# A dilated attention merge whose weights travel through DRAM instead of through TensorE

## The chip, the cores and the metric

The kernel runs on one core of a Trainium2 chip. The metric is the device time of one execution in microseconds. The core has a matrix engine (TensorE, PE in the profile), three engines for elementwise work (VectorE is DVE, ScalarE is ACT, GpSimd is POOL), a sync engine (SP) that issues the transfers, and 16 DMA engines that carry them out.

## The reference

The program is one layer of an encoder on 1024 positions of width 1024, in float32. What matters here is branch A, a dilated sliding-window attention with 8 heads of 64. It runs three window patterns, and merges them per position and head by their softmax denominators:

```python
def mixture_of_dilations(q, k, v, rel_bias):
    outs, lses = [], []
    for window, dilation in DIL_PATTERNS:          # (128,1), (512,4), (2048,16)
        o, lse = dilated_window_attention(q, k, v, rel_bias, window, dilation)
        outs.append(o)
        lses.append(lse)
    w = jax.nn.softmax(jnp.stack(lses, axis=0), axis=0)
    return jnp.einsum('gbsh,gbshd->bshd', w.astype(q.dtype), jnp.stack(outs, axis=0))
```

Branch B is a 2-D neighbourhood attention with 8 heads. Both branches are gated, projected and added to the residual; a feed-forward part with a depthwise convolution follows.

## The kernel before

Matrix products are made exact enough by splitting each float32 operand into a high and a low part, so one product step is three matmuls of 128x512 (lines L84 to L86, `product`). The program has these stages: a start with norms and the first projections, an attention loop, a gate stage, and the feed-forward part. The change lies in the attention loop.

**The slot loop.** The loop has 101 slots. Its order for TensorE, VectorE and ScalarE is written out by hand: `at(slot, phase, job)` puts a job into a slot, and each slot runs its phases in the order `first`, `O`, (fill), `T`, (fill), `late O`, `S`, `last`, (fill), `W`. Fill steps are product steps of the input projection, four in each of the slots 0 to 63, eight in 64 to 71, six in 72 to 87 and four after that; while they run, queued side work (evictions of results, splits of weights) is emitted as well. SP and GpSimd are not in that written order: a planner orders their instructions by its own simulation.

**The heads.** Dilated heads run in four pairs. Pair `pr` begins in slot 16·pr with its first head; the second head starts eight slots later. A pair's rows of the outputs `u` hold head 0 on partitions 0 to 63 and head 1 on 64 to 127. The pattern (128,1) is called near (group `g` = 0, tile `u1`), and the two dilated patterns are computed together and called far (`g` = 1, tile `u23`). Scores are made in `S`, the softmax (`softmax`, L580 and L581) runs on VectorE and ScalarE, the probabilities are transposed on TensorE in `T` into one of two PSUM buffers named T, and `split_t` (L588, L589) takes them out as high and low parts; a slot later they are multiplied with the values into a buffer O, which `finish` moves to `u`. Neighbourhood heads (`NaHead`) follow from slot 64 on, one each four slots, beside the end of pair 3.

**The merge.** The softmax leaves in `st` a negated maximum and a sum for each query row, for near (indices 0 and 1) and far (2 and 3). Near and far hold the queries in different orders on the partitions. Before the change this is how the weights come about:

- `exchange` (L799, slots 13 to 16 of the pair): 16 VectorE copies of 32x8 bring far's statistics into near's order, in `xs`.
- `factors` (L807 to L810, slot 16) and `shares` (L815 to L820, slot 17): the two weights per query, in `fa`.
- `give` (L825, slots 18 to 21): 16 VectorE copies bring far's weights back into far's order, in `fx`.
- `spread` (L830): GpSimd writes a quarter's weights 64 times, as `fw`, 128x512.
- `weigh` (L838, L840; slots 20, 21, 23, 24, phase `W`): TensorE transposes `fw` in four 128x128 blocks into a T buffer, and VectorE multiplies a quarter of `u` by it.
- `merge` (L847, L848, slot 25): GpSimd adds near to far, SP stores the pair to DRAM.

Of the kernel before, what the change touches and what calls it, by code (L numbers as in the profile page):

```python
# [10 lines left out]
FT = mybir.dt.float32  # L11
FR = mybir.dt.float32r
AF = mybir.ActivationFunctionType
OP = mybir.AluOpType
# [3 lines left out]
S = 1024  # L18
# [11 lines left out]
def hybrid_encoder(tc, xT, c, w_ada, small, w_in, p1_bias, p23_bias, na_bias, ln2_mult, ident, w_br, w_out,  # L30
                   w_up, w_down, out):
    nc = tc.nc
    act, dve, pool, pe, sp = nc.scalar, nc.vector, nc.gpsimd, nc.tensor, nc.sync
# [3 lines left out]
    dram = tc.alloc_tile_pool(name="scr", bufs=1, space=DRAM)  # L37
# [4 lines left out]
    idt = const.tile([128, 128], FT, name="idt")  # L42
# [186 lines left out]

    vb_c = dram.tile([S, 512], FT, name="vbc")  # L230
    g_scr = dram.tile([16, 128, S], FT, name="gs")
    o_scr = [dram.tile([4, 128, S], FT, name=n) for n in ("oa", "ob")]
    v_scr = dram.tile([S + 9 * 128, 512], FT, name="v")
    va_s, va_b = v_scr[:S], v_scr[S:].rearrange("(j p) n -> j p n", j=9)
# [147 lines left out]
    with tc.manual_schedule(engines={e.engine for e in (sp, act, dve, pool, pe)}):  # L382
        x = [x_load(0)]
# [16 lines left out]
        first = ps_s.tile([128, 512], FT, name="pv", bufs=3)  # L400
# [99 lines left out]
        for n, step in enumerate(v_steps[:9]):  # L500
# [14 lines left out]
            else:  # L515
                p = v_wide(*step[1:])
# [62 lines left out]
    def softmax(d, bias, pp, mi, li):  # L579
        dve.tensor_tensor_reduce(pp, d, bias, -1.0, BIG, OP.add, OP.min, mi)  # L580
        act.activation(pp, pp, AF.Exp, bias=mi, scale=-1.0, accum_out=li)  # L581
# [63 lines left out]
    def at(slot, phase, job, *args):  # L645
        slots[slot][phase].append((job, args))

    class DilHead:
# [22 lines left out]
        def load(self):  # L671
            loads[self.head] = dil_loads(self.head)
# [8 lines left out]
        def far_scores(self, r):  # L681
            qs, ks, kl, qb = qks[self.pr]
            ensure(qk_marks[self.pr])
            i, st = self.i, self.st()
            s = ps_l.tile([128, 512], FT, name="S")
            P = self.P[r] = sm_pool.tile([128, 2, 256], FT, name="P", bufs=5)
            for g in range(2):
                d = s[:, 256 * g:256 * g + 256]
                qc = slice(256 * r + 128 * g, 256 * r + 128 * g + 128)
                kc = slice(256 * r, 256 * r + 256)  # L690
                pe.matmul(d, qs[i][:, qc], ks[i][:, kc], start=True, stop=False)
                pe.matmul(d, qs[i][:, qc], kl[i][:, kc], start=False, stop=True)  # L692
            for g in range(2):
                d = s[:, 256 * g:256 * g + 256]
                e = 2 * r + g
                softmax(d, self.bt[:, 640 - 128 * g:896 - 128 * g], P[:, g], st[:, i, 2, e:e + 1], st[:, i, 3, e:e + 1])

        def far_turn(self, r):
            P = self.P.pop(r)
# [20 lines left out]
        def near_scores(self, n):  # L720
            qs, ks, kl, qb = qks[self.pr]
            ensure(qk_marks[self.pr])
            i, st = self.i, self.st()
            s = ps_l.tile([128, 512], FT, name="S")
            P = sm_pool.tile([128, 2, 256], FT, name="P", bufs=5)
            for x_ in range(2):
                b = 2 * n + x_
                t0, t1 = block_chunks(b)[0]
                d = s[:, 256 * x_:256 * x_ + 256]
                mid = t0 is not None and t1 is not None  # L730
                for dd, *keys in [(d, t0, 2)] if mid else [(d[:, 0:128], t0), (d[:, 128:256], t1)]:
                    pe.matmul(dd, qb[i][:, 128 * b:128 * b + 128], window(ks[i], *keys), start=True, stop=False)
                    pe.matmul(dd, qb[i][:, 128 * b:128 * b + 128], window(kl[i], *keys), start=False, stop=True)
            for x_ in range(2):
                b = 2 * n + x_
                off = block_chunks(b)[1]
                softmax(s[:, 256 * x_:256 * x_ + 256], self.bt[:, off:off + 256], P[:, x_], st[:, i, 0, b:b + 1],
                        st[:, i, 1, b:b + 1])
                self.P["near", b] = P[:, x_]

        def near_turn(self, js):
# [31 lines left out]
    class DilPair:  # L773
        def __init__(self, pr):
            self.pr, s0 = pr, 16 * pr
            at(s0, "first", self.begin) if pr else self.begin()
            for i in range(2):
                DilHead(self, pr, i, s0 + 8 * i, lambda: self.u, lambda: self.st)
            for r in range(4):
                at(s0 + 13 + r, "first", self.exchange, r)  # L780
                at(s0 + 18 + r, "first", self.give, r)
            at(s0 + 16, "last", self.factors)
            at(s0 + 17, "last", self.shares)
            for n, (g, z) in enumerate(((0, 0), (0, 1), (1, 0), (1, 1))):
                s = s0 + 18 + n + g
                at(s, "last", self.spread, g, z)
                at(s + 2, "W", self.weigh, g, z)
            at(s0 + 25, "first", self.merge)

        def begin(self):  # L790
            self.u = [at_pool.tile([128, S], FT, name=n) for n in ("u1", "u23")]
            self.st = sm_pool.tile([128, 2, 4, 8], FT, name="st")
            self.fw = {}

        def exchange(self, r):
            if r == 0:
                self.xs = at_pool.tile([128, 2, 2, 8], FT, name="xs")
            for q in range(4):
                dve.tensor_copy(self.xs[32 * r:32 * r + 32, :, :, q:8:4],  # L799
                                self.st[32 * q:32 * q + 32, :, 2:4, 2 * r:2 * r + 2])  # L800

        def factors(self):
            st, xs = self.st, self.xs
            fa = at_pool.tile([128, 2, 2, 8], FT, name="fa")
            fb = at_pool.tile([128, 2, 2, 8], FT, name="fb", bufs=1)
            fl = at_pool.tile([128, 2, 8], FT, name="fl", bufs=1)
            dve.tensor_tensor(fl, st[:, :, 0], xs[:, :, 0], OP.min)  # L807
            dve.tensor_tensor(fa[:, 0], fl, st[:, :, 0], OP.subtract)
            dve.tensor_tensor(fa[:, 1], fl, xs[:, :, 0], OP.subtract)
            act.activation(fa, fa, AF.Exp)  # L810
            self.fa, self.fb, self.fl = fa, fb, fl

        def shares(self):
            st, xs, fa, fb, fl = self.st, self.xs, self.fa, self.fb, self.fl
            dve.tensor_tensor(fb[:, 0], fa[:, 0], st[:, :, 1], OP.mult)  # L815
            dve.tensor_tensor(fb[:, 1], fa[:, 1], xs[:, :, 1], OP.mult)
            dve.tensor_tensor(fl, fb[:, 0], fb[:, 1], OP.add)
# [3 lines left out]
            self.fac = [fa[:, 0], at_pool.tile([128, 2, 8], FT, name="fx")]  # L821

        def give(self, r):
            for q in range(4):
                dve.tensor_copy(self.fac[1][32 * q:32 * q + 32, :, 2 * r:2 * r + 2],  # L825
                                self.fa[32 * r:32 * r + 32, 1, :, q:8:4])

        def spread(self, g, z):
            fw = self.fw[g, z] = at_pool.tile([128, 4, 2, 64], FT, name="fw")
            pool.tensor_scalar(fw, self.fac[g][:, :, 4 * z:4 * z + 4].rearrange("p i b -> p b i")  # L830
                               .rearrange("p b (i o) -> p b i o", o=1).to_broadcast([128, 4, 2, 64]), 1.0, None, OP.mult)

        def weigh(self, g, z):
            fw = self.fw.pop((g, z))
            ensure(self.done)
            pt = ps_a.tile([128, 512], FT, name="T")
            for b in range(4):
                pe.transpose(pt[:, 128 * b:128 * b + 128], fw[:, b], idt)  # L838
            dst = self.u[g][:, 512 * z:512 * z + 512]
            return lambda: dve.tensor_tensor(dst, dst, pt, OP.mult)  # L840

        def merge(self):
            u = self.u
# [8 lines left out]
    class NaHead:  # L852
# [15 lines left out]

        def load(self):
            if self.i == 0:  # L870
                oTs[self.head // 2] = at_pool.tile([128, S], FT, name="u1")
            self.st = at_pool.tile([128, 2, 8], FT, name="stb")
            self.vv = v_raw(vb_load, self.head)

# [896 lines left out]
```

## Time and profile before

| What | Value |
|---|---|
| Time, three runs | 1532.61, 1534.29, 1536.65 us; median 1534.29 |
| Profiled execution | 1535.67 us, of which its span is 1533.8 us |
| Busy, TensorE | 1494.4 us (97%) |
| Busy, VectorE | 994.6 us (65%) |
| Busy, ScalarE | 771.6 us (50%) |
| Busy, GpSimd | 774.2 us (50%) |
| DMA, mean over the span | 134 GB/s |

The profile is one execution. Its span runs from the first to the last instruction; the rest of the time lies around it. A row of a view names the line of the kernel, the engine, the operation, and the tiles written and read; in brackets may stand how long the engine was idle before it and who released it. PEld is the loading of weights into TensorE, which overlaps its matmuls. SPq is SP's queue; its rows give the time that an issue takes, not the transfer.

### The profile page before, as it was taken

The numbers are of one execution on the slowest core, as the hardware profiler recorded it, in microseconds if no ns is written. First come the engines' busy times: TensorE is split into PE (matmuls) and PEld (weight loads), VectorE is DVE, ScalarE is ACT, GpSimd is POOL, SyncE is SP. The second block draws the span as 40 slices with busy tenths as digits, with TensorE's granted clock in tenths as the row PEclk, the third lists the DMA queues.
The fourth block names the chain that finished last, engine by engine and source line by source line (L and its number), as shares of the span: only waits on it lengthen the run. The fifth ranks groups of instructions, "written<-read, shape, count | busy, mean of one in ns | idle before, by whom it ended". The sixth has DMA issues, their size and how long they took to land.

```text
span 1533.8 us, 21797 instructions
## 1 busy us (share of the span) xinstructions
PE 1494.4 (97%) x7740; PEld 1267.5 (83%) x7740; DVE 994.6 (65%) x1892; ACT 771.6 (50%) x1439; POOL 774.2 (50%) x640
## 2 busy tenths in 40 slices
PE   8999999999999999999999989999999998999998
PEld 7888888889798998878888867888888887778787
DVE  5775357575656655646525798766666668787765
ACT  4331566666656566643335463444444447475542
POOL 1021344443335444512268578676666666779721
PEclk9999999999999999999999999999999999999999
DMA  9567333333625456477644222222222224513313
GB/s 349 191 242 258 93 107 82 108 90 102 185 83 150 128 143 173 149 246 234 213 137 147 88 69 96 82 98 88 85 84 86 86 78 154 191 62 124 117 55 111
DMA packets 112725, 205.77 MB, mean 134 GB/s; under 512 B 40516, under 2 KB 53188, under 8 KB 112580
## 3 DMA queue, kind: packets, MB, share of 16 engines
q1 hardware_dynamic: 112344, 204.12, 41.2%
q8 instruction: 61, 1.00, 0.3%
q14 instruction: 48, 0.39, 0.1%
q10 hardware_dynamic: 272, 0.26, 0.1%
HBM read 159.25 MB, written 42.47 MB: 132 GB/s over the span
## 4 chain that ended last, share of the span: by engine, by line
PE 50%; POOL 8%; DVE 7%; ACT 3%; issue 3%; DMA 3%; DVEq 0%; POOLq 0%; ACTq 0%
PE pj L1204 8%; PE pj L1205 8%; PE pj L1206 8%; PE pj L84 6%; PE pj L86 6%; PE pj L85 6%; POOL wsl L61 2%; DMA wraw<-w_down 2%; PE pj L365 2%; PE O L932 2%; POOL wlo L61 2%; DVE big L1426 1%; PE T L919 1%; PE S L897 1%; DVE kl L340 1%
## 5 line engine op out<-in xcount | busy, mean ns | idle before, releaser
L61 POOL TENSOR_TENSOR wlo<-wraw,whi 128x512 fp32r<-128x512 f32 (+1 forms) x94 | 116.1, 1256 | 173.6 <-ACT whi L57 155.4
L84 PE MATMUL pj<-h,whi 128*128 128x512 f32 x448 | 186.7, 417 | 2.6 <-ACT h L207 2.2
L85 PE MATMUL pj<-h,whi 128*128 128x512 f32 x448 | 176.5, 394 | 2.1 <-DVE h L209 2.1
L86 PE MATMUL pj<-h,wlo 128*128 128x512 f32 x448 | 176.3, 393 | 0.0
L61 POOL TENSOR_TENSOR wsl<-big,wsh 128x512 fp32r<-128x512 f32 (+1 forms) x86 | 116.6, 1376 | 43.4 <-ACT wsh L57 43.4
L639 POOL TENSOR_TENSOR wlo<-wraw,whi 128x512 fp32r<-128x512 f32 x58 | 74.7, 1298 | 118.4 <-ACT whi L638 118.4
L589 DVE TENSOR_TENSOR tl<-T,th 128x512 fp32r<-128x512 f32 (+3 forms) x120 | 77.1, 653 | 72.9 <-ACT th L588 71.4
L581 ACT ACTIVATE P<-P,st 128x256 f32<-128x256 f32 x128 | 64.2, 502 | 95.9 <-DVE st L580 95.9
L1426 DVE SCALAR_TENSOR_TENSOR big<-wc,sm,big 128x256 f32<-128x256 f32 (+1 forms) x129 | 101.0, 827 | 15.1 <-ACT big L1420 15.1
L86 PEld LDWEIGHTS pj<-h,wlo 128*128 128x128 f32 x448 | 84.3, 188 | 18.7
L84 PEld LDWEIGHTS pj<-h,whi 128*128 128x128 f32 x448 | 85.0, 190 | 14.3 <-ACT h L207 2.8
L85 PEld LDWEIGHTS pj<-h,whi 128*128 128x128 f32 x448 | 85.0, 190 | 13.4 <-DVE h L209 3.4
L57 ACT ACTIVATE whi<-wraw 128x1024 fp32r<-128x1024 f32 (+2 forms) x51 | 49.5, 972 | 69.8 <-PE pj L85 26.7
L61 POOL TENSOR_TENSOR wsl<-wraw,wsh 128x384 fp32r<-128x384 f32 (+1 forms) x46 | 53.6, 1184 | 58.4 <-ACT wsh L57 58.3
L910 POOL TENSOR_SCALAR P<-P,stb 128x288 f32<-128x288 f32 (+1 forms) x32 | 40.2, 1255 | 72.2 <-DVE stb L907 64.7
L1426 DVE SCALAR_TENSOR_TENSOR big<-pj,sm,big 128x512 f32<-128x512 f32 (+1 forms) x129 | 66.4, 563 | 15.7 <-ACT big L1420 15.7
L588 ACT ACTIVATE th<-T 128x512 fp32r<-128x512 f32 (+3 forms) x120 | 65.6, 566 | 20.4 <-PE T L919 14.0
L57 ACT ACTIVATE wsh<-big 128x1024 fp32r<-128x1024 f32 (+1 forms) x43 | 42.9, 997 | 57.3 <-POOL big L1155 43.0
L547 POOL TENSOR_TENSOR vv<-vv 128x512 fp32r<-128x512 f32 (+1 forms) x40 | 41.9, 1065 | 47.2 <-ACT vv L546 47.2
L580 DVE CUSTOM_DVE_ANT_0 P<-S,bias 128x256 f32<-128x256 f32 x128 | 48.9, 419 | 21.4 <-PE S L692 17.0
L903 ACT ACTIVATE P<-P,stb 128x288 f32<-128x288 f32 (+1 forms) x64 | 36.4, 569 | 50.3 <-DVE stb L901 50.2
L1225 DVE TENSOR_TENSOR pj<-pj,wc 128x512 f32<-128x512 f32 x33 | 22.9, 695 | 53.1 <-PE pj L1206 53.1
(431 smaller groups left out, 4814.3 us busy)
## 6 DMA issues: line engine op xcount, KB each, us to landing
wraw<-w_in SPq DMA_DIRECT2D x34, 512.0 KB, 4.3
wada<-w_ada SPq DMA_DIRECT2D x31, 512.0 KB, 8.0
big<-w_up SPq DMA_DIRECT2D x22, 512.0 KB, 5.4
wraw<-w_up SPq DMA_DIRECT2D x22, 512.0 KB, 3.7
as<-big SPq DMA_DIRECT2D x22, 512.0 KB, 2.8
big<-as SPq DMA_DIRECT2D x22, 512.0 KB, 6.7
wraw<-w_down SPq DMA_DIRECT2D x24, 384.0 KB, 3.6
gs<-gs SPq DMA_DIRECT2D x32, 256.0 KB, 2.9
```

The source lines that it names most:

```text
L57: act.activation(hi, raw, AF.Copy)
L61: lo_eng.tensor_tensor(lo[:, i:i + step], raw[:, i:i + step], f(hi)[:, i:i + step], OP.subtract)
L84: pe.matmul(psum, whi[:, k0 + k], mhi, start=k == 0, stop=False)
L85: pe.matmul(psum, whi[:, k0 + k], mlo, start=False, stop=False)
L86: pe.matmul(psum, wlo[:, k0 + k], mhi, start=False, stop=k == n - 1)
L588: act.activation(th[:m, :n], pt[:m, :n], AF.Copy)
L589: dve.tensor_tensor(tl[:m, :n], pt[:m, :n], f(th)[:m, :n], OP.subtract)
L639: pool.tensor_tensor(lo[:, i:i + n], raw[:, i:i + n], f(hi)[:, i:i + n], OP.subtract)
L1204: pe.matmul(psum, whi[:, k], bhi, start=j < 4 and k == 0, stop=False, skip_group_check=True)
L1205: pe.matmul(psum, whi[:, k], blo, start=False, stop=False, skip_group_check=True)
L1206: pe.matmul(psum, wlo[:, k], bhi, start=False, stop=k == n - 1, skip_group_check=True)
L1426: dve.scalar_tensor_tensor(y[:, dst], src, wt, y[:, dst], OP.mult, OP.add)
```

## The change

The merge's weights no longer pass through VectorE copies, GpSimd and TensorE. Instead:

- `st` is laid out with the statistic first, and in slot 17 one TensorE transpose (`turn`) turns it to 64 rows of 128. `rows` copies them out of PSUM; SP stores them to a DRAM scratch (`st_scr`) and loads them back as `fs`, 64 partitions of 32 positions each, with nine loads that bring near and far into one order.
- `factors` and `shares` compute on 64x32 and move to slots 20 and 21. Afterwards `fa` goes to a second DRAM scratch (`f_scr`) with nine stores.
- A quarter's weights come back as `fb`, 128x512, by a transfer that reads each of the two heads' rows 64 times. Two buffers exist: far's quarters are loaded after `shares`, and near's as the far quarters free the buffers.
- `weigh` is one VectorE multiply of `u` by `fb`, in the phase `last` of slots 24, 26, 28 and 30, far first; `merge` moves from slot 25 to slot 31.
- `exchange`, `give` and `spread` are gone. The neighbourhood outputs, which took `u1` buffers, now take `u1` and `u23` in turn.

```diff
-                softmax(d, ..., st[:, i, 2, e:e + 1], st[:, i, 3, e:e + 1])
+                softmax(d, ..., st[:, 2, i, e:e + 1], st[:, 3, i, e:e + 1])
...
-            for r in range(4):
-                at(s0 + 13 + r, "first", self.exchange, r)
-                at(s0 + 18 + r, "first", self.give, r)
-            at(s0 + 16, "last", self.factors)
-            at(s0 + 17, "last", self.shares)
-            for n, (g, z) in enumerate(((0, 0), (0, 1), (1, 0), (1, 1))):
-                s = s0 + 18 + n + g
-                at(s, "last", self.spread, g, z)
-                at(s + 2, "W", self.weigh, g, z)
-            at(s0 + 25, "first", self.merge)
+            at(s0 + 17, "T", self.turn)
+            at(s0 + 20, "last", self.factors)
+            at(s0 + 21, "last", self.shares)
+            for n, (g, z) in enumerate(((1, 0), (1, 1), (0, 0), (0, 1))):
+                at(s0 + 24 + 2 * n, "last", self.weigh, g, z)
+            at(s0 + 31, "first", self.merge)
...
+        def turn(self):
+            pt = ps_a.tile([128, 512], FT, name="T")
+            pe.transpose(pt[:64, :128], self.st.rearrange("p s i b -> p (s i b)"), idt)
+            return lambda: self.rows(pt)
+
+        def rows(self, pt):
+            rows = at_pool.tile([64, 128], FT, name="fs", bufs=1)
+            dve.tensor_copy(rows, pt[:64, :128])
+            sp.dma_start(st_scr[self.pr], rows)
+            self.fs = at_pool.tile([64, 4, 32], FT, name="fs", bufs=1)
+            sp.dma_start(self.fs[:, 2:4], st_scr[self.pr][32:64].rearrange("(s x) (q j) -> (x q) s j", s=2, j=32))
+            near = st_scr[self.pr][0:32].rearrange("(s i b) (r j) -> i r b s j", s=2, i=2, r=4)
+            for i in range(2):
+                for r in range(4):
+                    sp.dma_start(self.fs[32 * i + 8 * r:32 * i + 8 * r + 8, 0:2], near[i, r])
...
+            to = f_scr[self.pr]
+            sp.dma_start(to[1].rearrange("i (x j) -> (i x) j", j=32), fa[:, 1])
+            near = to[0].rearrange("i (b r j) -> i r b j", b=8, r=4)
+            for i in range(2):
+                for r in range(4):
+                    sp.dma_start(near[i, r], fa[32 * i + 8 * r:32 * i + 8 * r + 8, 0])
+            self.fb = {}
+            for z in range(2):
+                self.load(1, z)
+
+        def load(self, g, z):
+            fb = self.fb[g, z] = at_pool.tile([128, 512], FT, name="fb")
+            sp.dma_start(fb, f_scr[self.pr, g][:, 512 * z:512 * z + 512].rearrange("i (o n) -> i o n", o=1)
+                         .to_broadcast([2, 64, 512]))
 
         def weigh(self, g, z):
-            fw = self.fw.pop((g, z))
             ensure(self.done)
-            pt = ps_a.tile([128, 512], FT, name="T")
-            for b in range(4):
-                pe.transpose(pt[:, 128 * b:128 * b + 128], fw[:, b], idt)
             dst = self.u[g][:, 512 * z:512 * z + 512]
-            return lambda: dve.tensor_tensor(dst, dst, pt, OP.mult)
+            dve.tensor_tensor(dst, dst, self.fb.pop((g, z)), OP.mult)
+            if g:
+                self.load(0, z)
```

More of the change, by code (lines that the diff above doesn't have):

```diff
@@ L231, in hybrid_encoder @@
     g_scr = dram.tile([16, 128, S], FT, name="gs")
+    st_scr = dram.tile([4, 64, 128], FT, name="sts")
+    f_scr = dram.tile([4, 2, 2, S], FT, name="fcs")
     o_scr = [dram.tile([4, 128, S], FT, name=n) for n in ("oa", "ob")]
@@ L695, in far_scores @@
                 e = 2 * r + g
[L696 removed]
+                softmax(d, self.bt[:, 640 - 128 * g:896 - 128 * g], P[:, g], st[:, 2, i, e:e + 1], st[:, 3, i, e:e + 1])
         def far_turn(self, r):
@@ L793, in begin @@
[L793 to L800, printed above, removed]
-        def factors(self):
[L803 to L809, printed above, removed]
+            self.st = sm_pool.tile([128, 4, 2, 8], FT, name="st")
@@ L810, in factors @@
+        def factors(self):
+            fs = self.fs
+            self.fa = fa = at_pool.tile([64, 2, 32], FT, name="fa", bufs=1)
+            self.fl = fl = at_pool.tile([64, 32], FT, name="fl", bufs=1)
+            dve.tensor_tensor(fl, fs[:, 0], fs[:, 2], OP.min)
+            for g in range(2):
+                dve.tensor_tensor(fa[:, g], fl, fs[:, 2 * g], OP.subtract)
             act.activation(fa, fa, AF.Exp)
-            self.fa, self.fb, self.fl = fa, fb, fl
         def shares(self):
-            st, xs, fa, fb, fl = self.st, self.xs, self.fa, self.fb, self.fl
@@ L815, in shares @@
-            dve.tensor_tensor(fb[:, 0], fa[:, 0], st[:, :, 1], OP.mult)
-            dve.tensor_tensor(fb[:, 1], fa[:, 1], xs[:, :, 1], OP.mult)
-            dve.tensor_tensor(fl, fb[:, 0], fb[:, 1], OP.add)
+            fs, fa, fl = self.fs, self.fa, self.fl
+            for g in range(2):
+                dve.tensor_tensor(fs[:, 2 * g], fa[:, g], fs[:, 2 * g + 1], OP.mult)
+            dve.tensor_tensor(fl, fs[:, 0], fs[:, 2], OP.add)
             dve.reciprocal(fl, fl)
@@ L870, in load @@
             if self.i == 0:
-                oTs[self.head // 2] = at_pool.tile([128, S], FT, name="u1")
+                oTs[self.head // 2] = at_pool.tile([128, S], FT, name=("u1", "u23")[self.head // 2 % 2])
             self.st = at_pool.tile([128, 2, 8], FT, name="stb")
```

14 lines of the change are left out of this document (2 added, 12 removed).

## The prediction

> **What bounds the kernel now.** I read the page first, for the engine that sets the end, then slices of the trace stage by stage, because the share of an engine over the whole span says nothing about the one stage that is edited.
>
> ```profile
> span 1533.8 us, 21797 instructions
> ...
> PE 1494.4 (97%) x7740; PEld 1267.5 (83%) x7740; DVE 994.6 (65%) x1892; ACT 771.6 (50%) x1439; POOL 774.2 (50%) x640
> ...
> PE 50%; POOL 8%; DVE 7%; ACT 3%; issue 3%; DMA 3%; DVEq 0%; POOLq 0%; ACTq 0%
> ```
>
> TensorE is 97% busy and carries half of the chain that ended last. Nothing else can shorten this kernel except through what TensorE is given to do or what it waits for. So each step below is priced by what it does to TensorE.
>
> The edited work lies in slots 12 to 24 of each head pair. In slots 0 to 63 a slot holds four fill steps of 12 wide matmuls in all, so the first wide matmul of every twelfth marks a slot's start. I counted them and asked for the same six slots at the same phase of the 16-slot period: slots 4 to 9, where no merge runs yet, and the six that hold a merge's weighing in pair 0 (20 to 25), pair 1 (36 to 41) and pair 2 (52 to 57). Columns: window, its length, busy time and count of TensorE, its weight loads, VectorE, ScalarE and GpSimd, granted clock, DMA share, GB/s.
>
> ```profile
> 173.50:198.90 25.40, 25.40 (x151) 22.00 (x150) 13.59 (x38) 17.47 (x45) 12.01 (x11) 1.00 0.32 84
> 242.10:269.90 27.80, 27.66 (x168) 23.51 (x166) 20.21 (x57) 17.98 (x46) 15.56 (x14) 1.00 0.29 75
> 313.10:340.90 27.80, 27.65 (x168) 23.50 (x166) 20.22 (x57) 17.98 (x46) 16.05 (x15) 1.00 0.28 74
> 384.20:415.30 31.10, 28.26 (x168) 23.29 (x167) 21.73 (x57) 19.74 (x45) 11.88 (x9) 1.00 0.62 169
> 469.80:510.20 40.40, 39.80 (x244) 35.12 (x245) 23.28 (x63) 21.34 (x50) 20.40 (x17) 1.00 0.52 149
> 528.60:561.30 32.70, 32.53 (x206) 29.07 (x205) 18.96 (x49) 20.60 (x46) 16.52 (x14) 1.00 0.64 184
> ```
>
> The first row is the price without the merge: 25.4 us. With it: 27.8, 27.8 and 31.1. Pair 3 is weighed in slots 68 to 72, beside neighbourhood heads (40.4 us); slots 76 to 80 are the same heads without it (32.7 us), with two fill steps fewer in each of four slots. The clock is 1.00 throughout, so these are waits and instructions, not throttling.
>
> **What the merge costs on TensorE, and so what leaves.** A close look at one group of four transposes, at a lone transpose, and at a wait:
>
> ```profile
> 246.00 0.39 PE L85 MATMUL pj<-h,whi 128*128 128x512 f32 x1
> ...
> 246.23 0.39 PE L86 MATMUL pj<-h,wlo 128*128 128x512 f32 x1
> ...
> 246.46 0.60 PE L838 MATMUL T<-idt,fw 128*128 128x128 f32 x4
> ...
> 247.13 0.40 PE L85 MATMUL pj<-h,whi 128*128 128x512 f32 x1
> ...
> 247.90 0.42 PEld L703 LDWEIGHTS T<-idt,P 128*128 128x128 f32 x4 [0.57 <-DVE tl L589]
> ```
>
> ```profile
> 232.77 0.39 PE L86 MATMUL pj<-h,wlo 128*128 128x512 f32 x1
> ...
> 233.00 0.27 PE L749 MATMUL T<-idt,P 128*128 128x128 f32 x1
> ...
> 233.35 0.40 PE L85 MATMUL pj<-h,whi 128*128 128x512 f32 x1
> ```
>
> ```profile
> PEld T L749 <- DVE tl L589: 3.0, 3, 2.1
> ```
>
> Wide matmuls start 0.23 us apart when nothing is between them (246.00, 246.23). From 246.23 to 247.13 lie two such steps and the group: 0.90 - 0.46 = 0.44 us for four transposes. The lone one: 0.58 - 0.46 = 0.12 us. The wait of 0.57 us at 247.90 is the second cost: a weighing takes one of the two T buffers, so the next slot's transposes must wait until VectorE has split the previous slot's. Without the weighing they need the buffer of two slots back. The last row (who waited for whom, 384 to 416 us) is the same wait in pair 2, longest 2.1 us.
>
> - Pairs 0 and 1: 27.8 - 25.4 = 2.4 us by the windows, 2.3 by the unrounded starts. 4 x 0.44 = 1.8 of it are transposes, the rest T waits. All of it goes: 2 x 2.3 = 4.6 us.
> - Pair 2: 31.1 - 25.4 = 5.7 us. 1.8 are transposes and about 3 T waits; the remainder follows slow strided evictions that stay. I take 4.2; ends 1.8 and 5.7.
> - Pair 3: the eight extra fill steps cost 8 x 3 x 0.23 = 5.5 us, so 40.4 - 32.7 - 5.5 = 2.2 us. I take 2.2; ends 1.8 and 2.6.
> - Added: one transpose per pair (`turn`), 0.12 us by the lone row, at most a group's 0.44: 4 x 0.12 = 0.5 us. It stands in slot 17 with two other T users, but those buffers were split a slot earlier.
>
> On TensorE: 4.6 + 4.2 + 2.2 - 0.5 = 10.5 us less.
>
> **What leaves and comes on VectorE and GpSimd.**
>
> ```profile
> L799 DVE COPY xs<-st x64: 162/167/306, 213.6 to 441.2; 32x8 f32<-32x8 f32 x64
> L825 DVE COPY fx<-fa x64: 146/161/1797, 235.8 to 479.9; 32x4 f32<-32x4 f32 x64
> L830 POOL TENSOR_SCALAR fw<-fx x8: 1485/1491/1505, 248.2 to 487.2; 128x512 f32<-128x512 f32 x8
> L840 DVE TENSOR_TENSOR u<-u,T x16: 673/684/687, 248.4 to 508.7; 128x512 f32<-128x512 f32 x16
> L1171 DVE TENSOR_TENSOR big<-big 128x512 f32<-128x512 f32 x10 | 15.9, 1589 | 1.2 <-POOL big L1155 1.2
> 268.33 0.69 DVE L589 TENSOR_TENSOR tl<-T,th 128x512 fp32r<-128x512 f32 x1 [1.22 <-ACT th L588]
> 271.14 0.68 DVE L624 TENSOR_TENSOR u<-O,u 64x512 f32<-64x512 f32 x1 [1.44 <-ACT u L623]
> ```
>
> 32 copies a pair leave VectorE (at least 32 x 0.16 = 5 us), and four spreads of 1.49 us leave GpSimd. Neither is on the path, as the 25.4 us row shows with VectorE only 13.6 us busy, so I book nothing for them; their room covers what comes. The factor arithmetic keeps its kind and shrinks to 64x32, about 0.17 us each. `rows` adds one small copy, hidden in VectorE's idle stretches of 1.2 to 1.4 us a slot (last two rows).
>
> The four weighings a pair stay on VectorE, but their second operand now comes from SBUF instead of PSUM. L840 has 0.68 us with T; L1171, with both operands in SBUF while GpSimd works, 1.59. I take 0.9 us, since GpSimd is busy 14 of 28 us here. The 0.2 us more per quarter fits in the idle stretches: nothing on TensorE; at worst 16 x 0.9 = 14.5 us of VectorE time, a quarter of which might show.
>
> The Trainium skill, "SBUF — State Buffer", section "SBUF: two separate sides", says that a VectorE operation with two SBUF inputs and a GpSimd operation that reads SBUF lock each other out for a whole instruction. By that rule, which speaks against this edit, a weighing could wait a whole GpSimd instruction; the L1171 row agrees.
>
> **The two round trips through DRAM.** They matter only if VectorE stands waiting, since all that is queued behind it (softmax, the split of T, evictions) feeds TensorE a slot later.
>
> ```profile
> 118.00:120.50 2.50, 2.50 (x12) 2.05 (x12) 2.40 (x5) 0.00 (x0) 0.00 (x0) 1.00 0.43 184
> ```
>
> ```profile
> out<-x SPq DMA_DIRECT2D x8, 128.0 KB, 1.9
> bias<-p_bias SPq DMA_DIRECT2D x8, 256.0 KB, 2.7
> ```
>
> ```profile
> 230.99 0.69 DVE L589 TENSOR_TENSOR tl<-T,th 128x512 fp32r<-128x512 f32 x1 [0.78 <-ACT th L588]
> ...
> 237.31 1.20 SPq L484 DMA_DIRECT2D vv<-v  x2
> ...
> 248.10 0.42 DVE L580 CUSTOM_DVE_ANT_0 P<-S,bias 128x256 f32<-128x256 f32 x1
> ...
> 251.23 0.35 SPq L65 DMA_DIRECT2D wraw<-w_in  x1
> ...
> 252.81 0.41 DVE L580 CUSTOM_DVE_ANT_0 P<-S,bias 128x256 f32<-128x256 f32 x1
> ...
> 266.09 0.42 DVE L580 CUSTOM_DVE_ANT_0 P<-S,bias 128x256 f32<-128x256 f32 x1
> ```
>
> The next two rows are of the w_in loads (source line L65): the spread of their times to landing, and what SP waited for in front of them between 160 and 560 us (total, times, longest).
>
> ```profile
> DMA to landing us min/median/max: 3.3/4.3/13.2
> ```
>
> ```profile
> SPq L65 <- POOL wlo L639: 82.3, 20, 14.0
> ```
>
> First trip: `rows` copies behind the split at 230.99, near 232 us; the store lands 1.9 us later (as the 128 KB `out` stores do), nine loads at 0.35 to 0.6 us of issue (L65, L484) take about 4, landing 2 more: 240 us, or 243 behind the next head's value loads (L484). `factors` runs after the softmax of slot 20, 248.5 us. No wait.
>
> Second trip: shares follow the softmax of slot 21, which ends at 253.2 us now and about 0.8 earlier then (the share of the 2.3 us that falls before it); seven small operations, 253.8. The far store goes first and lands by 256.0, the eight near stores hold SP until 257.5, then the two `fb` loads. Their source's outermost dimension is 2. The window from 118.0 to 120.5 us holds only transfers whose outermost dimension is 7 (`va_chunks`): DMA share 0.43, which is seven of 16 engines, at 184 / 7 = 26 GB/s each. On two engines 256 KB take 262144 B / (2 x 26 GB/s) = 5.0 us, and some 2 us of fixed time as the 1.9 us stores have: the first lands at 264.5 us, against 260.5 if it spread as the bias load does (2.7 us). The first weighing stands behind the softmax of slot 24, which ends at 266.4 now and 1.7 earlier then (the share of slots 20 to 23): 264.7. So it is just in time; the second quarter (5.0 us later, needed 9 us later) and the near quarters (12 us and more) have room. For a wait of 0 to 2 us, with about 3 us of slack before TensorE needs the next split, I book 1.0 us over all pairs; ends 0 and 4. The last pair's loads also run beside the neighbourhood bias loads; that is inside the 4.
>
> The Trainium skill, "DMA: Bandwidth & Descriptors", section "Rules for kernel authors", says that a leading outermost dimension smaller than 16 confines a DMA to that many engines, which speaks against this change. The trace agrees: 0.43 is seven engines.
>
> **Sum.** -10.5 + 1.0 = -9.5 us. The profiled execution took 1535.67 us (span 1533.8 and 1.9 around it), 1.4 above the median of 1534.29. So 1526.2 in its terms, 1524.8 us as a median. What comes after the stage is TensorE-bound with its loads ahead of it, so I let the whole gain through. Own range of this case: -12.4 (all of pair 2 and 2.6 in pair 3, no wait) and some 3 us of reordering by the planner, to -4.6: 1519 to 1529.7.
>
> **Rivals.**
> - *Slower: the first far quarter lands late.* Its place is the first `weigh` of each pair, on VectorE, in order. For it: SP is one queue, its order is the planner's, and a w_in load stood there 14.0 us for GpSimd (last row); and one of those loads, issued behind the seven-engine transfers, took 13.2 us to land. Against it: SP issues nothing from 238.5 (L484) to 251.2 us (L65), and that wait ends before the shares are ready. Each us beyond about 3 costs TensorE one, in four pairs. At 8 us late: 4 x 5 = 20, less 10.5: 1543.8 us. It decides from 6.8 us on, (10.5 + 4.6) / 4 + 3. Chance 0.16.
> - *No change: VectorE becomes the bound.* Every weighing takes 1.59 us and the T waits come back as waits for late splits. Then only the transposes go, 16 x 0.44 = 7.0, less 0.5, less a quarter of 14.5: 2.9 us less, 1531.4. For it: 20.2 of 27.8 us busy; against: 5 us of copies leave. Chance 0.14.
> - *The spread uses all engines after all.* No wait anywhere: 1523.8. It is inside the forecast's 0.70.
>
> **Numbers.** About 0.3% (4.6 us) is what a measurement of this kernel can tell from no change. Faster 0.70, same 0.14, slower 0.16. The range, 1519 to 1537, takes in the no-change case and the mild end of the slow one.
>
> **What would show it.** Right: the six slots of pairs 0 and 1 take about 25.5 us; no T wait for VectorE's split after 242 us; L838's transposes gone; weighings of 0.7 to 1.6 us; two DMA engines busy for 5 us per `fb` load. Wrong: VectorE idle behind an `fb` DMA for more than 3 us, a small `sts` or `fcs` transfer issued late on SP, or a TensorE wait in slots 20 to 32 that was not there.

## The result and the profile after

| | before | after |
|---|---|---|
| Median of the timed runs beside each other | 1533.47 us (4 runs, 1532.61 to 1536.65) | 1522.81 us (4 runs, 1520.40 to 1526.79) |
| Ratio, 95% interval | | 0.9934 [0.9919, 0.9949] |
| Profiled execution | 1535.67 us | 1522.23 us |

The change makes the kernel faster by 10.7 us by the medians (forecast: 9.5 against the median shown then). First the page of the kernel after.

```profile
span 1520.5 us, 21650 instructions
...
PE 1484.7 (98%) x7680; PEld 1263.0 (83%) x7680; DVE 964.0 (63%) x1768; ACT 770.2 (51%) x1439; POOL 751.7 (49%) x624
...
PE 77%; DMA 6%; DVE 6%; POOL 5%; ACT 3%; issue 2%; SPq 0%; DVEq 0%; POOLq 0%; ACTq 0%
```

TensorE's 60 instructions fewer are the 64 transposes less the four of `turn`; VectorE loses 124 instructions and 31 us, GpSimd 16 and 22.5 us. TensorE now carries 77% of the chain that ended last. Now the stretches of the kernel after that answer to those shown of before, with their columns: slots 4 to 9, 20 to 25, 36 to 41, 52 to 57, 68 to 72 and 76 to 80. The bounds are those of before, carried over by matching the sequence of TensorE's matmuls in the two traces.

```profile
173.40:198.80 25.40, 25.40 (x151) 22.00 (x149) 13.59 (x38) 17.44 (x45) 12.02 (x11) 1.00 0.33 84
242.20:267.70 25.50, 25.50 (x152) 22.06 (x150) 15.63 (x50) 17.81 (x47) 11.03 (x10) 1.00 0.28 72
311.10:336.60 25.50, 25.50 (x152) 22.05 (x150) 15.57 (x50) 17.81 (x47) 11.02 (x10) 1.00 0.32 81
379.90:407.50 27.60, 25.84 (x151) 22.04 (x150) 15.91 (x46) 19.33 (x45) 6.96 (x6) 1.00 0.72 192
462.90:500.70 37.80, 37.80 (x229) 33.49 (x228) 19.17 (x59) 21.36 (x51) 18.07 (x15) 1.00 0.58 161
519.20:551.80 32.60, 32.43 (x205) 29.01 (x204) 21.69 (x51) 20.52 (x46) 19.34 (x16) 1.00 0.70 200
```

Pairs 0 and 1 take 25.5 us where 27.8 stood, as a stage without any merge does (25.4). Pair 2 takes 27.6 instead of 31.1, and pair 3 37.8 instead of 40.4. Pair 2 gives 1.2 us of its 3.5 back one slot later:

```profile
409.81 0.28 PE L768 MATMUL O<-tl,vv 128*128 128x256 f32 x1
411.04 0.33 PE L768 MATMUL O<-th,vv 128*128 128x128 f32 x1 [0.94 <-ACT th L590]
```

From the loop's start to slot 98 the kernel after gains 9.3 us. The profiled executions differ by 13.4. Some 3 us of the rest lie between 1300 and 1420 us of the span, where the traces of all the changed kernels, whatever they changed in the loop, are 0.4 to 4.6 us ahead of that one execution of before; so that is not counted for the change.

The weights' road is seen best in who waited for whom (160 to 660 us), in the rows of `fb`, in one window of 2.5 us, and in SP's queue:

```profile
DVE u L843 <- DMA fb<-fcs: 12.7, 6, 3.7
...
PE O L768 <- DVE tl L591: 1.8, 1, 1.8
PE O L768 <- ACT th L590: 0.9, 1, 0.9
```

```profile
L837 SPq DMA_DIRECT2D fb<-fcs x16: 499/544/1848, 255.6 to 510.6; - x16
L843 DVE TENSOR_TENSOR u<-u,fb x16: 684/692/1310, 264.5 to 535.7; 128x512 f32<-128x512 f32 x16
```

```profile
257.50:260.00 2.50, 2.50 (x15) 2.08 (x14) 2.00 (x6) 1.38 (x5) 2.50 (x4) 1.00 0.13 51
```

```profile
255.58 1.16 SPq L837 DMA_DIRECT2D fb<-fcs  x2
256.84 2.72 SPq L347 DMA_DIRECT2D ks<-ks  x1
...
264.57 6.43 SPq L347 DMA_DIRECT2D kl<-kl  x2
...
272.23 0.56 SPq L837 DMA_DIRECT2D fb<-fcs  x1
...
274.38 5.94 SPq L484 DMA_DIRECT2D vv<-v  x1
...
284.12 0.53 SPq L837 DMA_DIRECT2D fb<-fcs  x1
```

```profile
264.53 0.69 DVE L843 TENSOR_TENSOR u<-u,fb 128x512 f32<-128x512 f32 x1 [0.19 <-DMA fb<-fcs]
271.69 0.69 DVE L843 TENSOR_TENSOR u<-u,fb 128x512 f32<-128x512 f32 x1
281.84 0.69 DVE L843 TENSOR_TENSOR u<-u,fb 128x512 f32<-128x512 f32 x1 [1.54 <-DMA fb<-fcs]
292.21 0.69 DVE L843 TENSOR_TENSOR u<-u,fb 128x512 f32<-128x512 f32 x1 [3.75 <-DMA fb<-fcs]
```

A weighing takes 0.69 us at the median, 1.31 at most. While the two far loads are under way the DMA share is 0.13, two of 16 engines, at 51 / 2 = 26 GB/s each: the transfers are as narrow as forecast. The first far quarter lands at 264.5 us, as forecast, and VectorE waits 0.19 us for it. That it came to the tenth is luck: the load took 8.9 us from its issue instead of 7.0, and SP issued it 1.9 us earlier than forecast (255.58 instead of 257.5). VectorE waits longer for the near quarters, 1.54 and 3.75 us, since their loads, issued at 272.23 and 284.12, take 8 to 10 us. Meanwhile some of SP's other issues stretch: a key transfer takes 2.72 us to issue, a value transfer 5.94. (The row of 6.43 us holds two issues of 0.46 us each, with a wait between them.) TensorE has no wait there.

### The profile page after: what moved, and what is told of

It reads as the page before. It is cut to its first block, busy times and chain, and to the rows that moved or that the text cites. A ratio compares the mean times of both kernels' runs of the same rounds, so it can differ in the third digit from the quotient of the medians.

```text
span 1520.5 us, 21650 instructions
## 1 busy us (share of the span) xinstructions
PE 1484.7 (98%) x7680; PEld 1263.0 (83%) x7680; DVE 964.0 (63%) x1768; ACT 770.2 (51%) x1439; POOL 751.7 (49%) x624
## 4 chain that ended last, share of the span: by engine, by line
PE 77%; DMA 6%; DVE 6%; POOL 5%; ACT 3%; issue 2%; SPq 0%; DVEq 0%; POOLq 0%; ACTq 0%
PE pj L84 10%; PE pj L86 10%; PE pj L85 10%; PE pj L1209 10%; PE pj L1210 10%; PE pj L1211 10%; PE pj L367 3%; PE O L937 2%; DMA wraw<-w_down 1%; POOL wsl L61 1%; DVE big L1431 1%; PE T L924 1%; PE S L902 1%; DMA fb<-fcs 1%; PE O L768 1%
## 5 line engine op out<-in xcount | busy, mean ns | idle before, releaser
L583 ACT ACTIVATE P<-P,st 128x256 f32<-128x256 f32 x128 | 64.2, 502 | 94.3 <-DVE st L582 94.3
L1457 ACT ACTIVATE big<-big 128x1024 f32<-128x1024 f32 x22 | 23.3, 1061 | 65.3 <-DVE big L1431 65.3
```

## The experiments

Each kernel was timed beside the kernel before, whose medians in these jobs were 1533.3 to 1535.3 us. "Loop" is what a kernel's profiled execution gains (minus) or loses on that of before from the loop's start to slot 98; for the kernel after it is -9.3 us.

| kernel | median, us | ratio to before, 95% interval | loop, us |
|---|---|---|---|
| e1 transposes back | 1529.64 | 0.9981 [0.9970, 0.9992] | -4.0 |
| e2 transposes held | 1529.00 | 0.9976 [0.9966, 0.9986] | -4.0 |
| e6 before, no transposes | 1529.76 | 0.9975 [0.9964, 0.9987] | -3.4 |
| e7 before, no copies | 1528.24 | 0.9970 [0.9960, 0.9981] | -4.8 |
| e8 before, no spreads | 1530.66 | 0.9978 [0.9967, 0.9990] | -1.8 |
| e11 before, no copies, no transposes | 1519.56 | 0.9904 [0.9889, 0.9920] | -9.9 |
| e3 wide loads | 1523.80 | 0.9930 [0.9914, 0.9946] | -9.6 |
| e4 narrow early | 1546.29 | 1.0084 [1.0067, 1.0100] | +14.0 |
| e5 wide early | 1533.34 | 0.9999 [0.9986, 1.0011] | -0.4 |
| e9 copies back | 1531.99 | 0.9978 [0.9964, 0.9993] | -2.1 |
| e10 copies back, wide | 1529.95 | 0.9970 [0.9958, 0.9982] | -3.4 |
| e12 copies later, wide | 1524.95 | 0.9938 [0.9921, 0.9956] | -8.4 |

### What leaves TensorE

**e1**, the kernel after with four transposes of the identity in each slot where a weighing stood:

```diff
+            for s in (20, 21, 23, 24):
+                at(s0 + s, "W", self.extra)
...
+        def extra(self):
+            pt = ps_a.tile([128, 512], FT, name="T")
+            for b in range(4):
+                pe.transpose(pt[:, 128 * b:128 * b + 128], idt, idt)
+            return lambda: None
```

> The changed kernel, with four idle transposes of the identity put back on TensorE in each of the four slots (20, 21, 23, 24) where the weighing stood; nothing reads them, so no T buffer is held. Theory A (the gain is TensorE's own work and its waits for T buffers): 16 x 0.44 = 7.0 us come back, 1529.8 us against 1522.8, the T waits stay away. Theory B (the gain is VectorE's relief from 128 small copies and GpSimd's from the spreads): TensorE has room for them, within 2 us of 1522.8.

Measured 6.8 us slower than the kernel after by the medians, 5.3 in the loop. In pairs 0, 1 and 3 the four groups cost 1.8 us a pair, so 0.44 us a group is confirmed there. In pair 2 they cost 0.1 us in all: there TensorE's two waits for splits, 1.8 and 0.9 us in the kernel after, give way to one T wait of 1.4.

**e2** adds a reader, so that each group also holds its T buffer until VectorE comes to it:

```diff
-            return lambda: None
+            return lambda: dve.tensor_copy(pt[:, 0:8], pt[:, 8:16])
```

> As e1, and a VectorE copy of 8 columns reads each group, so that the T buffer is held until VectorE comes to it, as the weighing held it. Theory A: the T waits come back on top of the 7.0 us, 2 to 4 us more, 1532 to 1534 us, which is the kernel before. Theory B: no more than e1 plus the small copies, 1523 to 1526 us.

Measured the same as e1, which is neither theory's number. TensorE has no T wait between 236 and 380 us (pairs 0 and 1), though each group takes a T buffer and VectorE has to free it. So holding the buffer is not enough for the T waits of the kernel before; VectorE must be late besides. The small copy frees the buffer sooner than the 0.68 us multiply did; e7 has the multiply itself. In pair 2 (380 to 420 us) e2 has the T wait of e1, and e7 has one of 1.2 us.

**e6**, the kernel before, weighing with `fw` as it lies in SBUF:

```diff
-            pt = ps_a.tile([128, 512], FT, name="T")
-            for b in range(4):
-                pe.transpose(pt[:, 128 * b:128 * b + 128], fw[:, b], idt)
...
-            return lambda: dve.tensor_tensor(dst, dst, pt, OP.mult)
+            return lambda: dve.tensor_tensor(dst, dst, fw.rearrange("p b i o -> p (b i o)"), OP.mult)
```

> The kernel before with one edit: the weighing multiplies by the spread factors where they lie in SBUF, without the four transposes and without a T buffer, so the weights meet the wrong elements. The copies and the spreads stay. Theory A: nearly the whole gain, 9 to 11 us less than before (1522.5 to 1524.5 us). Theory B: at most 3 us less, 1530.5 us or more.

Measured 3.5 us less: a third of what theory A named, and a little over theory B's 3. Slots 20 to 25 do get 2.2 us shorter, but slot 26 gets 1.4 us longer, and slot 42 again. The wait, in the view of who waited for whom (TensorE, 236 to 380 us; the kernels before, e1, e2 and after have no such row there):

```profile
PE O L766 <- ACT th L588: 1.9, 2, 1.0
```

**e7**, the kernel before without `exchange` and `give`; far's numbers are read where they lie:

```diff
-                at(s0 + 13 + r, "first", self.exchange, r)
-                at(s0 + 18 + r, "first", self.give, r)
+                pass
...
-            st, xs = self.st, self.xs
+            st = self.st
+            self.xs = xs = st[:, :, 2:4]
...
-            self.fac = [fa[:, 0], at_pool.tile([128, 2, 8], FT, name="fx")]
+            self.fac = [fa[:, 0], fa[:, 1]]
```

> The kernel before with one edit: the 32 VectorE copies a pair (exchange and give) are left out, so far's statistics and weights stay in their own order. Spreads, transposes and T buffers stay. Theory A: 0 to 2 us less than before (1531.5 to 1533.5 us), the 2 only where pair 3's copies of up to 2.9 us made TensorE wait. Theory B: 5 us less or more, 1528.5 us or less.

The copies, which the prediction booked at nothing, are worth 5.0 us by themselves, 4.8 in the loop: 0.5 in each of pairs 0 and 1, 2.3 in pair 2 and 1.5 in pair 3. In pairs 0 and 1 just the T waits go, with the multiply still holding the buffers: slots 20 to 25 get 0.45 us shorter and end where e1's do.

**e8**, the kernel before without GpSimd's spreads; the transposes take the identity:

```diff
-                at(s, "last", self.spread, g, z)
...
-                pe.transpose(pt[:, 128 * b:128 * b + 128], fw[:, b], idt)
+                pe.transpose(pt[:, 128 * b:128 * b + 128], idt, idt)
```

> The kernel before with one edit: GpSimd's 16 spreads are left out, and the weighing's transposes take the identity instead of fw, so the weights are wrong. Copies, transposes and T buffers stay. Theory C (VectorE's 32 copies a pair cost TensorE by their number): no gain, 1532 to 1534 us. Theory L (the copies were slow, up to 2.85 us for four, because a spread held the port they need): the copies of give fall to 0.16 us each and the time by 2 to 4 us, 1529.5 to 1531.5 us.

3.4 us by the medians, 1.8 in the loop of the profiled execution. The interval of the ratio allows 1.5 to 5 us, so theory L's number is met but not sharply. Its mechanism shows in part: `give`'s copies over 0.2 us are gone in pairs 0 to 2, while three of pair 3 stay (0.68 to 1.80 us). In pairs 0 and 1 the T waits nearly go here too (0.4 us a pair): the softmax of slot 21 is 1.4 us late instead of 2.5, by the count explained below.

**e11** has e7's and e6's edits together:

> The kernel before without the 32 VectorE copies a pair and without the 64 transposes; GpSimd's spreads stay and the weighing multiplies by the spread weights as they lie (so the weights are not the right ones). Alone the copies gave 5.0 us and the transposes 3.5 us against a base of 1533.3. Theory A (the two waits take each other's place: with both gone the transposes are worth their full 7.0 us of TensorE and the T waits go too): 9.5 to 11 us less, 1522.5 to 1524.5, like the kernel after. Additive theory: 8.5 us less, 1525. Theory G (GpSimd's spreads are the other half of the trouble, since they lock VectorE's weighing of two SBUF operands): 5 to 7 us less, 1526.5 to 1529, with waits of TensorE for split T behind weighings of over 1 us.

14 us by medians (four runs between 1519 and 1524), 9.9 in the loop, more than the kernel after gains there. Apart 3.5 + 5.0 by the medians and 3.4 + 4.8 in the loop, together more than the sum by either: theory A, whose 9.5 to 11 us holds the loop's figure, while the median lies beyond it. The rows of TensorE's waits for `th` are gone from 236 to 380 us, with GpSimd's spreads still there; theory G falls.

### The road of the weights

**e3** splits each `fb` load by head, so that its outermost dimension is 64:

```diff
-            sp.dma_start(fb, f_scr[self.pr, g][:, 512 * z:512 * z + 512].rearrange("i (o n) -> i o n", o=1)
-                         .to_broadcast([2, 64, 512]))
+            for i in range(2):
+                sp.dma_start(fb[64 * i:64 * i + 64], f_scr[self.pr, g][i:i + 1, 512 * z:512 * z + 512]
+                             .to_broadcast([64, 512]))
```

> The changed kernel, with each fb load split by head, so that its source's outermost dimension is 64 instead of 2. Theory N (the transfers run on two engines, and VectorE's 12.7 us of waits on them are hidden behind its slack): the loads land in 3 us, VectorE's waits on fb go to zero, SP's stretched issues (2.7 us for one k copy) come back to 0.55 us, and the time moves by 2 us at most, 1521 to 1523 us. Rival W (those waits still reach TensorE): 4 us less or more, 1519 us or less.

No gain that shows. Yet the waits are gone, and the two long issues are short again (0.54 and 0.60 us); the group of the weighings (idle time before them last) and the same stretch of SP's queue:

```profile
L844 DVE TENSOR_TENSOR u<-u,fb 128x512 f32<-128x512 f32 x16 | 12.5, 782 | 0.0
```

```profile
256.12 0.54 SPq L347 DMA_DIRECT2D ks<-ks  x1
...
261.52 0.56 SPq L347 DMA_DIRECT2D kl<-kl  x1
```

So the 12.7 us that VectorE waited in the kernel after were covered, and the narrow transfers cost it nothing.

**e4**, the kernel after with the weighings two slots earlier:

```diff
-                at(s0 + 24 + 2 * n, "last", self.weigh, g, z)
-            at(s0 + 31, "first", self.merge)
+                at(s0 + 22 + 2 * n, "last", self.weigh, g, z)
+            at(s0 + 29, "first", self.merge)
```

> The changed kernel with the weighings two slots earlier (22, 24, 26, 28; merge in 29), the narrow loads unchanged. It tests the prediction's price of a late quarter. By the prediction: the first quarter is wanted 8.6 us before it lands, about 3 us of it are slack, so TensorE loses 5 us in each of four pairs, 1522.8 + 20 = 1543 us. Rival S (VectorE's slack is larger, since its waits of 3.7 us in the changed kernel left no mark on TensorE): 1525 to 1533 us.

Measured 1546.29 us, near the 1543.8 of the prediction's slower rival, whose mechanism this is. VectorE waits once in each pair, 5.7 to 9.9 us, and in the loop the four pairs lose 23 us against the kernel after; the rival had 20. But pairs 0 to 2 lose 7.0 to 8.5 us each and pair 3 only 0.6. VectorE first, TensorE second:

```profile
262.01 0.69 DVE L843 TENSOR_TENSOR u<-u,fb 128x512 f32<-128x512 f32 x1 [8.12 <-DMA fb<-fcs]
```

```profile
263.95 0.58 PE L768 MATMUL O<-tl,vv 128*128 128x256 f32 x1 [4.52 <-DVE tl L591]
```

**e5** is e4's edit with e3's wide loads.

> The kernel after with each weight load split into one transfer per head, and the four weighings at slots 22, 24, 26 and 28 as in the narrow early kernel. Theory N (the early kernel lost 23 us because a narrow transfer lands some 7 us after its issue and holds the next ones up): a wide transfer lands in about 2.7 us, the first far quarter is there near 260 us against a wanted 256, the later ones are in time: VectorE waits for a weight load 4 us or less in pair 0, and the median is 1522 to 1530 us. Rival P (the early place itself is bad, as the weighing falls into the wrong slots of VectorE's order, whatever the width): 1538 us or more, as the narrow early kernel had 1546.29.

Neither: 13 us better than e4, 10 us worse than wide loads in the old place. VectorE waits only 3.35 us in pair 0, within what theory N allowed (1.3 to 5.4 us over the pairs), but TensorE pays in slots 25 and 26:

```profile
259.42 0.69 DVE L844 TENSOR_TENSOR u<-u,fb 128x512 f32<-128x512 f32 x1 [3.35 <-DMA fb<-fcs]
```

```profile
266.09 0.33 PE L768 MATMUL O<-tl,vv 128*128 128x128 f32 x1 [0.35 <-DVE tl L591]
...
272.16 0.33 PE L768 MATMUL O<-th,vv 128*128 128x128 f32 x1 [0.95 <-ACT th L590]
```

The second matmul comes three slots after the wait. Why a wait of slot 22 is paid in slot 26 was open then; the next three kernels settle it.

### The copies and their place

**e9**, the kernel after with 32 VectorE copies a pair, in place, where `exchange` and `give` stood:

```diff
+            for r in range(4):
+                at(s0 + 13 + r, "first", self.extra, 8)
+                at(s0 + 18 + r, "first", self.extra, 4)
...
+        def extra(self, n):
+            flat = self.st.rearrange("p s i b -> p (s i b)")
+            for q in range(4):
+                part = flat[32 * q:32 * q + 32, 32:32 + n]
+                dve.tensor_copy(part, part)
```

> The changed kernel with 32 VectorE copies a pair put back in the phases and slots where exchange and give stood (13 to 16 and 18 to 21), each a copy of far's statistics onto themselves. No spreads, no transposes. Theory C: the copies cost what leaving them out of the kernel before gave, 3 to 5 us, 1526 to 1528 us. Theory L: 0.16 us each without a spread to wait for, inside VectorE's slack, at most 1 us, 1522.5 to 1524 us.

9 us slower than the kernel after by the medians, 7.3 in the loop, more than either theory. I took this for the copies and the waits for the near quarters adding up, and tried it without those waits.

**e10** has e9's copies and e3's wide loads.

> The kernel after with the 32 in-place VectorE copies a pair back, and with weight loads split into one transfer per head, so that VectorE waits for no weight load. With narrow loads the copies cost 9 us (1531.99). Theory W (the copies' 5 to 6 us a pair of VectorE time and the waits for narrow near quarters add up; either alone is covered): 1522.5 to 1526 us, and no wait of TensorE over 0.6 us in slots 26 to 32. Theory C (VectorE's room in the loop is used up by the copies alone): 1527 to 1530 us, with TensorE waits for split T (0.6 us and more) beside the copies' slots.

1529.95 us: theory W falls, since no weighing waits for a load, and TensorE waits all the same, in e6's place:

```profile
PE O L768 <- ACT th L590: 1.9, 2, 1.0
```

Around that matmul in pair 0, all engines in order of time:

```profile
268.29 0.69 DVE L591 TENSOR_TENSOR tl<-T,th 128x512 fp32r<-128x512 f32 x1 [1.22 <-ACT th L590]
268.37 0.27 PE L751 MATMUL T<-idt,P 128*128 128x128 f32 x1
268.89 0.41 DVE L582 CUSTOM_DVE_ANT_0 P<-S,bias 128x256 f32<-128x256 f32 x1
...
269.35 0.51 ACT L583 ACTIVATE P<-P,st 128x256 f32<-128x256 f32 x1 [1.10 <-DVE st L582]
...
271.59 0.76 ACT L590 ACTIVATE th<-T 128x128 fp32r<-128x128 f32 x2
...
271.91 0.33 PE L768 MATMUL O<-th,vv 128*128 128x128 f32 x1 [0.96 <-ACT th L590]
```

The block that TensorE transposed at 268.37, as the last job of slot 25, is multiplied half a slot later, in slot 26; other blocks have a whole slot and more. ScalarE could take it from 268.64, but its order puts the previous slot's exponentials (L583) and two evictions of 0.6 us first. The exponentials wait for VectorE's softmax (268.89), and that stands behind a split (268.29) which waited for ScalarE.

The waits for the near quarters are the smaller part of e9's loss: it is 2.0 us slower than e10 by the medians, 1.3 in the loop, most of it in slots 32 to 34.

**e12** moves the second set of e10's copies behind that place:

```diff
-                at(s0 + 18 + r, "first", self.extra, 4)
+                at(s0 + 26 + r, "first", self.extra, 4)
```

> The kernel with the copies back and weight loads split per head (1529.95), but with the second set of 16 copies a pair at slots 26 to 29 instead of 18 to 21. The count of VectorE instructions is the same. Theory L (lateness: VectorE and ScalarE hand each slot's softmax back and forth, a chain about as long as TensorE's slot, so that what VectorE is late by in slots 18 to 25 is carried to slot 26, where TensorE has to wait once it is more than about 2 us; in the traces the softmax of slot 24 is 1.5 us late in the wide kernel and 2.7 us late with the copies): with the copies behind slot 26 the softmax of slot 24 is 1.3 to 1.7 us late again, TensorE has no wait in slot 26, and the median is 1522.5 to 1526 us. Theory C (the amount of VectorE work in the loop counts): 1528 to 1531 us, as before the move.

1524.95 us, and the same work is nearly free: theory L. In the loop it costs 1.1 us against e3, nearly all in slots 76 to 80. The same rows:

```profile
264.04 0.69 DVE L591 TENSOR_TENSOR tl<-T,th 128x512 fp32r<-128x512 f32 x1 [1.22 <-ACT th L590]
...
264.65 0.42 DVE L582 CUSTOM_DVE_ANT_0 P<-S,bias 128x256 f32<-128x256 f32 x1
...
265.49 0.27 PE L751 MATMUL T<-idt,P 128*128 128x128 f32 x1
...
267.35 0.76 ACT L590 ACTIVATE th<-T 128x128 fp32r<-128x128 f32 x2
...
267.93 0.22 PE L768 MATMUL O<-th,vv 128*128 128x128 f32 x1
```

From the transpose to `th` it is 1.86 us here and 3.22 in e10; of the difference of 1.36, TensorE waited 1.13 by the spacing of its matmuls (0.96 in its row).

The softmax's lateness shows it for pair 0. It is the start of a slot's first softmax operation, counted from the slot's first fill matmul, less the same figure 16 slots earlier, where no merge runs (the expectation of e12 gave 1.5 and 2.7 for slot 24, where this count has 0.55 and 1.99):

| lateness, us | slot 19 | 20 | 22 | 23 | 24 | slot 26 longer by |
|---|---|---|---|---|---|---|
| e3 | 0.50 | 0.48 | 0.57 | 0.55 | 0.55 | 0 |
| after | 0.50 | 0.49 | 0.59 | 0.57 | 0.56 | 0 |
| e11 | 0.49 | 0.45 | 0.46 | 0.46 | 0.46 | 0 |
| e12 | 0.53 | 0.52 | 0.66 | 0.65 | 0.64 | 0 |
| e10 | 1.91 | 1.89 | 1.99 | 1.99 | 1.99 | 1.4 |
| e6 | 2.12 | 2.09 | 2.10 | 2.10 | 2.10 | 1.4 |
| e5 | 0.50 | 0.49 | 0.59 | 2.53 | 2.52 | 1.4, slot 25 by 0.5 |
| before | 2.12 | 2.09 | 1.65 | 1.45 | 1.09 | 0 |

What VectorE is late by is carried from slot 19 to slot 24 undiminished. The brackets above show how: VectorE and ScalarE hand each slot's work to and fro and wait for each other (1.22, 1.10 us), and that a delay neither grows nor dies out says that this chain is as long there as TensorE's slot, though both engines look half idle. Slot 26 collects what exceeds some 0.6 us (1.99 less 1.4; 2.52 less 1.9). In the kernel before the lateness shrinks on the way, because there TensorE pays in other coin, in transposes and T waits. In e12 the lateness is 0.6 to 2.0 us in slots 26 to 32, and nothing collects it. The table is of pair 0; in pair 1, slot 42 is longer by the same 1.4 us in e10, e6 and e5. In pairs 2 and 3, where most of e7's 5.0 us lies, the chain was not followed slot by slot, so there the account is not shown.

## Why the prediction was right, and where not

- *Pairs 0 and 1, 2 x 2.3 us*: right in size (27.8 to 25.5). The transposes' 0.44 us is confirmed by e1. The step that explained the T waits, "a weighing takes one of the two T buffers", was half the cause: e2 and e7 hold the buffers and have none there. The other half is VectorE's lateness, which the copies make (e7) and the spreads raise (e8).
- *Pair 2, 4.2 us*: 3.5 in its window and 1.2 given back, net 2.3. It fell between the ends given. The wait that came back is slot 26's kind, `O` on `th`. *Pair 3, 2.2*: 2.6, the upper end. *`turn`, 0.5*: slot 17 is 0.13 us longer in pair 0, as the lone transpose said.
- The sum of these, with the forecast's 0.5 for `turn`, is 4.6 + 2.3 + 2.6 - 0.5 = 9.0 us, against 10.5 forecast and 9.3 from the loop's trace. The 1.4 us between the loop and the medians stay unassigned; they lie within the spread of the runs.
- *Waits for `fb`, 1.0 us*: VectorE waited 12.7 us and TensorE paid nothing (e3). The first landing was forecast to the tenth by two errors that cancel: the load took 8.9 us, not 7.0, and was issued 1.9 us early. "The near quarters (12 us and more) have room" failed: they were the late ones, because their load is issued when a far quarter frees its buffer and a two-engine transfer issued then takes 8 to 10 us. One of the forecast's own signs of being wrong, "VectorE idle behind an `fb` DMA for more than 3 us", so came true (3.75 us). It cost nothing: the softmax is 2.3 us late in slot 31, and slots 31 to 33 are as long as in e3. In e9, where it is 3.2 us late there, slots 32 to 34 are 0.3 to 0.5 us longer each than in e10, so that place has its limit too.
- *Weighing, 0.9 us*: 0.69, 1.31 at most. The term was too dear because few weighings meet GpSimd at work. Only three of the 16 began while one of its instructions ran, and each ended 0.55 us after that instruction's end (1.31, 1.09 and 0.69 us). The Trainium skill, "SBUF — State Buffer", section "SBUF: two separate sides", says that a VectorE operation with two SBUF inputs and a GpSimd operation that reads SBUF lock each other out for a whole instruction. The trace agrees in these three, and in e6 one weighing took 1.53 us in the same way. The weighing of 1.31 us and the GpSimd instruction before it:

```profile
496.88 1.30 POOL L641 TENSOR_TENSOR wlo<-wraw,whi 128x512 fp32r<-128x512 f32 x1
497.42 1.31 DVE L843 TENSOR_TENSOR u<-u,fb 128x512 f32<-128x512 f32 x1
```

- *Copies and spreads "at nothing"*: the step that failed. "VectorE only 13.6 us busy" of 25.4 was read as room. It is not: the copies alone cost 5.0 us (e7). In pairs 0 and 1 the reason is shown: a chain through two engines was full while each engine was half idle. The total came out right since the change removes copies and transposes together, so that the T waits that I had booked did go, for another reason. Where only the transposes were removed, the same account gave 9 to 11 us, and 3.5 came (e6).
- *"About 3 us of slack"*: too much. It is about 0.6 us for a lateness that reaches slot 26, and the kernel after arrives there with 0.56. The slower rival's mechanism is real and its sum was near (23 us for 20, e4), though partly by luck: the loss in pairs 0 to 2 was larger and in pair 3 smaller than its 5 us a pair. Its threshold was nearer than thought: first quarters 1.3 to 5.4 us late lose already nearly the whole gain (e5).

## What to carry to other kernels

Room on an engine is not its idle share: where two engines hand work to and fro once a slot, look for the start of the same step from slot to slot, and see whether a delay dies out or is carried to a consumer. Then place extra work behind the consumer that collects it; here the same 16 copies a pair, moved behind it, gave 5 us back. When two removals are judged one at a time, each can be half hidden by the other, so judge them together as well.

## What the runs showed of the hardware

- Transfers on two DMA engines held up some of SP's other issues: while an `fb` load was under way, one key transfer took 2.72 us to issue and one value transfer 5.94; with the loads split by head (e3) the same two took 0.54 and 0.60. Others issued beside an `fb` load took 0.46 to 0.55 us as usual.
- Small VectorE copies of 32x4 took 0.16 us each mostly, up to 1.80 for one in the kernel before. What stretches them is GpSimd at work: each of the 13 copies of `give` over 0.2 us began while a GpSimd instruction ran and ended 0.01 to 0.04 us after the end of one. Seven others began under a spread and took 0.16 us, so not every copy waits. Without the spreads (e8), ten of the 13 are gone. One of the 13:

```profile
249.92 1.28 POOL L639 TENSOR_TENSOR wlo<-wraw,whi 128x512 fp32r<-128x512 f32 x1 [0.25 <-ACT whi L638]
250.05 1.18 DVE L825 COPY fx<-fa 32x4 f32<-32x4 f32 x1
```
